# A trunk kernel on one Trainium2 core: another order in its plain norm tiles, its passage to attention as a step list, and a softmax that takes the query latent's root

## The chip, the cores and the metric

The kernel runs on one core of one Trainium2 chip. The metric is the device time of one execution in microseconds (us).

## The reference

Two layers on x of 1024 tokens by 1024 features: layer 0 mixes by a short gated convolution, layer 1 by multi-head latent attention, and both end in a squared-ReLU MLP. Every sublayer has a norm before it and one behind it:

```python
h = modulate(rmsnorm(x, norm_g[l, 0]), sh_m, sc_m)
y = short_conv_mixer(...) if l < N_A else mla_mixer(...)
x = x + g_m[:, None, :] * rmsnorm(y, norm_g[l, 1])
h = modulate(rmsnorm(x, norm_g[l, 2]), sh_f, sc_f)
x = x + g_f[:, None, :] * rmsnorm(squared_relu_mlp(h, w_up, w_down), norm_g[l, 3])
# attention, 8 heads; c_kv and k_pe are made once from x after layer 0
c_kv = rmsnorm(kv_a[..., :256], kv_a_norm_g); k_pe = apply_rope(kv_a[..., 256:], cos, sin)
q = rmsnorm(h @ q_a_w, q_a_norm_g) @ q_b_w      # 384 latent channels, per head 128 + 64 rotary
s = (qn @ k_nope.T + qp @ k_pe.T) / sqrt(192)   # masked by chunks of 64, then softmax, then @ v
```

## The kernel before, in words

A float32 product is three fp32r matmuls of a high and a low part (`mm`, L168 to L170), and `split_w` (L172 to L174) makes the parts: ACT copies the high part, DVE subtracts for the low one. A matmul is 128x128 by 128x512.

**Seams.** Where a sublayer ends, its down product comes as eight tiles of 128 tokens by 1024 features, 24 matmuls each, into one of two 128x1024 PSUM tiles (`big`). `Seam.tile` (L309 to L317) adds a tile to y (DVE), squares and sums it (ACT, L255), takes the root (ACT L257, DVE L262), scales (DVE L315), adds to x (DVE L316), stores x (L317), and squares the new x; `flush` (L295, ACT) makes the pre-norm for the next product. The sequence on each engine is pinned to the written one. At three places a seam stands between stages: behind the convolution (about 344 to 392 us of the trace), behind the first MLP (from 977.6 us), behind attention (1467 to 1516 us). The first and third write five plain tiles and run the rest by a hand-written list, `ORDER`, in which the transposes for the next product (L418), their splits (L429, L430) and its first matmuls are mixed with the last tiles. The last seam of the kernel keeps its order in both kernels.

**Passage to attention** (977.6 to 1116.1 us). All eight tiles are plain ones. `h_steps` transposes the pre-normed tokens (PE L484), scales them (ACT L486) and splits them (DVE L490, L491). `first_block` multiplies half the tokens by the query latent's weights; `latent` (L1311 to L1321) copies each product out of PSUM, squares it, sums over channels with a 128x512 product against ones (L1315), takes root and reciprocal of all 128x512 sums (L1316, L1317), scales by it and by the gain (L1319) and splits. It is done for both halves of the query latent and both of the key latent; `rotary_keys` makes the rotary key.

**Attention** (1116.1 to 1467 us, heads from 1160). Per head come eight score tiles (`scores`, 128 queries by up to 1024 keys): matmuls into `big` (L1471), a mask (L1472), the negated row maximum (DVE L1474), Exp with the maximum as bias and a running sum (ACT L1477), reciprocal (L1481), scaling (L1482), transposes and splits of the probabilities (`turn`, L1497 to L1501) and the products with the values. Ahead of the first head stand `queries`, `rotary` and `keys` for both halves. Background steps (`run_bg`, modulation vectors, DVE L195) are spread over it; outside the pinned stretches a scheduler orders the engines.

## Time and profile before

| | |
|---|---|
| median of 3 runs | 2141.66 us (2141.5 to 2142.57) |
| the profiled execution | 2144.59 us, its span 2142.8 us |
| granted TensorE clock, mean | 0.996 |
| busy: PE, PEld, DVE, ACT | 97%, 80%, 72%, 49% |
| seam behind the convolution, 344.6 to 391.8 us | PE busy 45.59 of 47.2 us |
| passage, 977.6 to 1116.1 us | PE busy 131.5 of 138.5 us |
| start of attention, 1116.1 to 1160 us | PE busy 38.78, DVE 41.49 of 43.9 us |
| heads, 1160 to 1412 us | PE busy 243.93, DVE 193.35 of 252 us |

PE is TensorE's matmuls and PEld its weight loads, which overlap them; DVE is VectorE, ACT ScalarE. A row of the timeline is start, duration, engine, line, operation, the tiles written and read, and in brackets the idle time before it with the engine that ended it. A busy PE is not PE at its peak, since pipelined matmuls overlap.

### The profile page before, as it was taken

What the parts mean: (1) busy time and instruction counts of PE and PEld (TensorE: products, weight loads), DVE (VectorE), ACT (ScalarE), POOL (GpSimd) and SP (SyncE); (2) the same over time, 40 slices, a digit from 0 to 9 for tenths busy, and PEclk for the clock granted to TensorE, in tenths of its full rate; (3) what the DMA queues carried; (4) which work ended last, traced back from release to release, by engine and by line L of the source; (5) the groups of instructions that cost most, each with busy time, mean ns of one, the idle gap of its engine ahead of it and who ended that gap; (6) DMA issues with size and microseconds to landing.
All of it is one profiled execution on the core that took longest, in us unless ns stands there. A gap on an engine that the chain in (4) does not pass through costs nothing.

```text
span 2142.8 us, 25254 instructions
## 1 busy us (share of the span) xinstructions
PE 2083.0 (97%) x9638; PEld 1715.1 (80%) x9638; DVE 1532.3 (72%) x2066; ACT 1060.5 (49%) x1512; POOL 4.0 (0%) x8
## 2 busy tenths in 40 slices
PE   5999999999999999999899999999999999999998
PEld 4888888888888878888777878877888888888887
DVE  5877776977665668876788877766977665558556
ACT  4533353845444434344665555564845444444342
POOL 0000000000000000000000000000000000000000
PEclk9999999999999999999999999999999999999999
DMA  8344454466443976465214231043455543853343
GB/s 245 95 147 146 131 200 136 133 192 215 157 152 131 326 230 226 151 210 178 81 59 124 78 106 44 26 149 132 129 184 184 183 166 134 300 191 122 98 147 138
DMA packets 242336, 330.85 MB, mean 154 GB/s; under 512 B 18630, under 2 KB 143907, under 8 KB 242215
## 3 DMA queue, kind: packets, MB, share of 16 engines
q1 hardware_dynamic: 204328, 248.57, 37.2%
q10 hardware_dynamic: 37886, 80.67, 10.0%
q8 instruction: 76, 1.25, 0.2%
q14 instruction: 46, 0.37, 0.0%
HBM read 248.45 MB, written 80.74 MB: 154 GB/s over the span
## 4 chain that ended last, share of the span: by engine, by line
PE 75%; DVE 12%; ACT 6%; DMA 5%; issue 2%; ACTq 0%; SPq 0%; DVEq 0%
PE one L170 40%; PE mm L170 19%; PE tp L170 7%; PE big L170 3%; ACT junk L255 2%; DMA raw<-in_ada_w_dram 2%; PE big L1471 2%; DVE y L315 1%; DVE raw L316 1%; DVE acc L195 1%; PE tp L1497 1%; DVE small L1474 1%; DVE y L309 1%; DVE pt L1501 1%; ACT small L257 1%
## 5 line engine op out<-in xcount | busy, mean ns | idle before, releaser
L170 PE MATMUL one<-slot,uphi 128*128 128x512 f32 x1240 | 381.9, 389 | 0.0
L170 PEld LDWEIGHTS one<-slot,uphi 128*128 128x128 f32 x1240 | 232.8, 188 | 48.7 <-issue 0.5
L170 PE MATMUL big<-slot 128*128 128x512 f32 x1152 | 267.6, 392 | 0.9 <-DVE slot L174 0.6
L170 PEld LDWEIGHTS big<-slot 128*128 128x128 f32 x1152 | 216.0, 189 | 47.7 <-ACT y L924 1.0
L170 PE MATMUL one<-slot,uplo 128*128 128x512 f32 x620 | 243.0, 392 | 1.6 <-DVE y L584 1.6
L173 ACT ACTIVATE ring<-w 128x1024 fp32r<-128x1024 f32 x98 | 103.8, 1059 | 267.1 <-PE tp L170 145.7
L170 PE MATMUL one<-ring,ring 128*128 128x512 f32 x1008 | 229.5, 389 | 0.3 <-DVE ring L174 0.3
L170 PEld LDWEIGHTS one<-ring,ring 128*128 128x128 f32 x1008 | 189.2, 188 | 40.0 <-DVE ring L174 0.7
L174 DVE TENSOR_TENSOR ring<-w,ring 128x1024 fp32r<-128x1024 f32 x98 | 119.8, 1222 | 122.8 <-ACT ring L173 122.6
L174 DVE TENSOR_TENSOR uplo<-raw,uphi 128x1024 fp32r<-128x1024 f32 x117 | 142.7, 1222 | 79.1 <-ACT uphi L173 79.0
L173 ACT ACTIVATE uphi<-raw 128x1024 fp32r<-128x1024 f32 x117 | 123.7, 1059 | 136.1 <-PE one L170 77.4
L170 PE MATMUL mm<-ring,ring 128*128 128x512 f32 x672 | 163.1, 391 | 2.4 <-DVE ring L174 2.4
L170 PE MATMUL tp<-ring,ring 128*128 128x512 f32 x672 | 161.8, 389 | 0.0
L170 PE MATMUL mm<-slot,uphi 128*128 128x512 f32 x504 | 157.9, 394 | 0.5 <-DVE slot L430 0.5
L170 PEld LDWEIGHTS mm<-ring,ring 128*128 128x128 f32 x672 | 125.6, 188 | 29.7 <-DVE ring L174 3.5
L170 PEld LDWEIGHTS tp<-ring,ring 128*128 128x128 f32 x672 | 126.1, 188 | 26.2
L170 PEld LDWEIGHTS one<-slot,uplo 128*128 128x128 f32 x620 | 116.4, 188 | 26.5 <-DVE y L584 2.4
L195 DVE SCALAR_TENSOR_TENSOR acc<-raw,csil,acc 128x1024 f32<-128x1024 f32 x88 | 112.4, 1277 | 35.1 <-DMA raw<-in_ada_w_dram 32.5
L174 DVE TENSOR_TENSOR ring<-raw,ring 128x1024 fp32r<-128x1024 f32 x98 | 119.3, 1218 | 10.7 <-ACT ring L173 10.7
L170 PE MATMUL one<-slot,s 128*128 128x512 f32 x468 | 114.0, 393 | 0.7 <-DVE s L174 0.7
L170 PEld LDWEIGHTS mm<-slot,uphi 128*128 128x128 f32 x504 | 94.8, 189 | 21.1 <-issue 1.4
L582 ACT ACTIVATE y<-one 128x512 f32<-128x512 f32 x62 | 36.7, 592 | 143.5 <-PE one L170 114.3
(272 smaller groups left out, 3487.0 us busy)
## 6 DMA issues: line engine op xcount, KB each, us to landing
ha<-y ACTq DMA_DIRECT2D x196, 256.0 KB, 3.0
raw<-ha SPq DMA_DIRECT2D x98, 512.0 KB, 4.3
raw<-in_ada_w_dram SPq DMA_DIRECT2D x80, 512.0 KB, 4.4
raw<-in_mlp_up_w_dram SPq DMA_DIRECT2D x70, 512.0 KB, 4.9
w<-in_mlp_down_w_dram SPq DMA_DIRECT2D x56, 512.0 KB, 4.8
raw<-hd SPq DMA_DIRECT2D x24, 512.0 KB, 4.3
xs<-raw ACTq DMA_DIRECT2D x24, 512.0 KB, 3.1
raw<-xs SPq DMA_DIRECT2D x24, 512.0 KB, 4.2
```

What stands on the lines that cost most here:

```text
L170: nc.tensor.matmul(out_, lhs[a], rhs[b], start=first and i == 0, stop=last and i == 2, skip_group_check=more)
L173: nc.scalar.activation(hi, src, AF.Copy)
L174: nc.vector.tensor_tensor(lo, src, hi.bitcast(F32), op=ALU.subtract)
L195: nc.vector.scalar_tensor_tensor(acc, raw, s, acc, op0=ALU.mult, op1=ALU.add)
L255: nc.scalar.activation(junk, src, AF.Square, accum_out=ss)
L257: nc.scalar.activation(rt, ss, AF.Sqrt, bias=eps_d)
L309: nc.vector.tensor_tensor(y, y, p_, op=ALU.add)
L315: nc.vector.scalar_tensor_tensor(y, y, rroot(ss), self.gmb, op0=ALU.mult, op1=ALU.mult)
L316: nc.vector.tensor_tensor(xr, xr, y, op=ALU.add)
L582: nc.scalar.activation(dst, x_, AF.Copy)
L1471: nc.tensor.matmul(o_, a, m_, start=j == 0, stop=j == 4)
L1474: nc.vector.tensor_reduce(mx, sp[:, :n], AX.X, ALU.max, negate=True)
```

## The change

1. **Plain tiles.** `Seam.tile` adds, squares y, then does the x addition, store and square of the *previous* tile, scales its own tile, and last makes the previous tile's pre-norm. The two list-run seams have it in their first five tiles.
2. **Passage.** `LATENTS`, a list of named steps in pinned order, takes the place of `h_steps`, `first_block`, `latent` and `rotary_keys`: the last three tiles of the seam (`mm5`, `add5` ...), transposes (`tr`), scaling (`tu`), splits (`sp`), blocks of the query product (`f`, `g`, `e`), the key product (`v`, `k`). Query products of the second half lie in `big`.
3. **Query latent's root.** It is no longer multiplied into the latent. The squares are summed with 128x1 products against ones into a column per 128 tokens, `rsq`, with sqrt(192) folded in; the gain is applied where the product leaves PSUM. `scores` multiplies the negated maximum by `rsq` (a 128x1 DVE instruction, 64 in all) and gives it to Exp as scale.
4. **Key latent's root.** Also from 128x1 products, root and reciprocal on 128x4, then spread over 128x512 by four transposes of a broadcast column.
5. **Start of attention.** Keys of half 0 and values 0 and 1 are written ahead of the queries of half 0; `run_bg(5)` is written as 0 for head 0.
6. The epsilons lie in one 128x8 tile; masked scores are -2^120.

```diff
 SLOTS = 6
 AHEAD = 5
+LATENTS = """
+mm5 tr0_0 tr0_1 add5 tu0_0 mm6 tu0_1 sq5 sp0_0 sp0_1 stt5 tr0_2 rc4 xad5 tr0_3 pre4 mm7 add6 tu0_3 dma5 tu0_2 sp0_3
+sq6 sp0_2 sqx5 stt6 tr0_4 rc5 xad6 pre5 tr0_5 f0 add7 tu0_5 dma6 sqx6 sp0_5 tr0_6 f1 mul7 sq7 rc6 pre6 f2 stt7 tu0_4
...
 """.split()
 VEC_ROWS = 109
@@ -152,10 +166,11 @@
     ones = cp.tile([P, P], F32, name="ones")
     nc.vector.memset(ones, 1.0)
-    eps_d = cp.tile([P, 1], F32, name="eps_d")
-    nc.vector.memset(eps_d, D * EPS)
-    eps_1 = cp.tile([P, 1], F32, name="eps_1")
-    nc.vector.memset(eps_1, EPS)
+    eps = cp.tile([P, 8], F32, name="eps")
+    eps_d, eps_1, eps_q = (eps[:, i:i + 1] for i in range(3))
+    for e, v in ((eps_d, D * EPS), (eps_1, EPS), (eps_q, (NOPE + ROPE) * EPS)):
+        nc.vector.memset(e, v)
+    rsq = cp.tile([P, NT], F32, name="rsq")
     nc.scalar.activation(small(), eps_1, AF.Sqrt)
     vecs = cp.tile([P, VEC_ROWS], F32, name="vecs")
...
         def flush(self):
             if self.rest is not None:
-                y, xr, ss = self.rest
-                nc.scalar.activation(y, xr, AF.Copy, scale=rroot(ss))
+                t, y, xr = self.rest
+                nc.vector.tensor_tensor(xr, xr, y, op=ALU.add)
+                nc.scalar.dma_start(self.xdst[t * P:(t + 1) * P, :], xr)
+                self.ss = None if self.last else squares(self.nx, xr)
+        def tail(self):
+            if self.rest is not None and not self.last:
+                t, y, xr = self.rest
+                nc.scalar.activation(y, xr, AF.Copy, scale=rroot(self.ss))
             self.rest = None
-        def tile(self, t, p_, steps):
+        def tile(self, t, p_):
             y = self.ys[t]
             if t == 0:
                 return
             with pinned():
                 nc.vector.tensor_tensor(y, y, p_, op=ALU.add)
-                self.back()
                 ss = squares(self.nx, y)
+                if not self.last:
+                    self.flush()
+                nc.vector.scalar_tensor_tensor(y, y, rroot(ss), self.gmb, op0=ALU.mult, op1=ALU.mult)
+                self.tail()
+                self.rest = (t, y, xr)
+                if self.last:
+                    self.flush()
+        def acts(self, first):
+            with pinned():
                 self.flush()
-                if t >= 5:
-                    self.front(steps, 2)
-                nc.vector.scalar_tensor_tensor(y, y, rroot(ss), self.gmb, op0=ALU.mult, op1=ALU.mult)
-                nc.vector.tensor_tensor(xr, xr, y, op=ALU.add)
-                nc.scalar.dma_start(self.xdst[t * P:(t + 1) * P, :], xr)
-                if not self.last:
-                    self.rest = (y, xr, squares(self.nx, xr))
-        def acts(self, first):
-            acts, ss, sx, rs = {}, {}, {first - 1: self.rest[2]}, {}
+            acts, ss, sx, rs = {}, {}, {first - 1: self.ss}, {}
             self.load(first + 2)
...
-    def h_steps(tp, ys, half, key, dst):
...
-    def first_block(seam, steps0, steps1, ws, h):
...
-    def latent(h, hf, ws, g, dst, steps=None, firsts=None):
...
-    def rotated(p_, hf, scale, stab, z, y):
+    def rotated(p_, hf, stab, z, y):
         sl = slice(hf * HALF, (hf + 1) * HALF)
         for i in range(4):
             j = i ^ 1
-            nc.scalar.activation(y[32 * i:32 * i + 32, :], p_[32 * j:32 * j + 32, :], AF.Copy, scale=scale)
-        nc.vector.scalar_tensor_tensor(z, p_, scale, ctab[:, sl], op0=ALU.mult, op1=ALU.mult)
+            nc.scalar.activation(y[32 * i:32 * i + 32, :], p_[32 * j:32 * j + 32, :], AF.Copy)
+        nc.vector.tensor_tensor(z, p_, ctab[:, sl], op=ALU.mult)
         nc.vector.tensor_tensor(y, y, stab[:, sl], op=ALU.mult)
...
+    def latents(seam, ws, ys):
+        acts = seam.acts(PLAIN)
...
+        def turn(fam, hf, k):
+            p_ = tp_ps()
+            for t in range(4):
+                nc.tensor.transpose(p_[:, t * P:(t + 1) * P], ys[hf * 4 + t][:, k * P:(k + 1) * P], ident)
+            t_[fam, k] = p_
...
+        def rooms(hf):
+            if hf == 0:
+                t_["big"] = big_ps()
+                return [mm_ps(), mm_ps(), t_["big"][:, :HALF]]
+            return [t_["big"][:, HALF:], *halves(big_ps())]
+        def block(hf, k):
+            if k == 0:
+                out_[hf] = rooms(hf)
+            for p_, w in zip(out_[hf], ws):
+                part_of(p_, w, hf, k)
+        def rest(m):
+            for k in range(4, KD):
+                part_of(out_[1][m], ws[m], 1, k)
...
+        def q_high(hf, m):
+            nc.scalar.activation(qaT[0][:, m, half(hf)], out_[hf][m], AF.Copy, scale=gq[:, m:m + 1])
+        def q_low(hf, m):
+            nc.vector.scalar_tensor_tensor(qaT[1][:, m, half(hf)], out_[hf][m], gq[:, m:m + 1], qaT[0][:, m, half(hf)].bitcast(F32),
+                                           op0=ALU.mult, op1=ALU.subtract)
+        def q_square(hf, m):
+            nc.scalar.activation(sq_of(hf, m), out_[hf][m], AF.Square)
+        def add_squares(key):
+            a, b = t_["sq", key]
+            nc.vector.tensor_tensor(a, a, b, op=ALU.add)
+        def token_sums(p_, sq):
+            for t in range(4):
+                nc.tensor.matmul(p_[:, t:t + 1], sq[:, t * P:(t + 1) * P], ones[:, 0:1], start=True, stop=True)
...
+        def q_sums(hf):
+            p_ = t_["qs", hf] = big_ps() if hf else mm_ps()
+            token_sums(p_, t_["sq", hf][0])
+        def q_root(hf):
+            nc.scalar.activation(rsq[:, 4 * hf:4 * hf + 4], t_["qs", hf][:, :4], AF.Sqrt, scale=(NOPE + ROPE) / QL, bias=eps_q)
...
+        def q_inverse(hf):
+            nc.vector.reciprocal(rsq[:, 4 * hf:4 * hf + 4], rsq[:, 4 * hf:4 * hf + 4])
...
+        def k_product(hf, m):
+            p_ = out_["k", hf, m] = big_ps()[:, :HALF] if m == 2 else mm_ps()
+            for k in range(KD):
+                part_of(p_, wk[m], hf, k)
...
+        def k_sums(hf):
+            p_ = t_["vs", hf] = big_ps()
+            token_sums(p_, t_["sq", "k", hf][0])
...
+        def k_root(hf):
+            rs = t_["vr", hf] = small(4)
+            nc.scalar.activation(rs, t_["vs", hf][:, :4], AF.Sqrt, scale=1.0 / KL, bias=eps_1)
...
+        def k_spread(hf):
+            for t in range(4):
+                nc.tensor.transpose(t_["vs", hf][:, HALF + t * P:HALF + (t + 1) * P], t_["vr", hf][:, t:t + 1].to_broadcast([P, P]), ident)
+        def k_norm(hf, m):
+            a = t_["raw", hf][m]
+            nc.vector.scalar_tensor_tensor(a, a, gk[:, m:m + 1], t_["vs", hf][:, HALF:], op0=ALU.mult, op1=ALU.mult)
...
+        with pinned():
+            for name in LATENTS:
+                acts[name]()
+        return t_["qw"], t_["kw"]
+    qw_, kw = latents(seam, ws, ys)
...
     def queries(Q, qw_, hf):
         p_ = project(qw_, slice(0, P), qaT, 3, hf)
         Q[hf] = part(at, "q", 3, [P, HALF])
-        nc.scalar.activation(Q[hf][0], p_, AF.Copy, scale=SM)
-        nc.vector.scalar_tensor_tensor(Q[hf][1], p_, SM, Q[hf][0].bitcast(F32), op0=ALU.mult, op1=ALU.subtract)
+        nc.scalar.activation(Q[hf][0], p_, AF.Copy)
+        nc.vector.tensor_tensor(Q[hf][1], p_, Q[hf][0].bitcast(F32), op=ALU.subtract)
     def rotary(R, qw_, hf, room=mm_ps):
         z, y = (at.tile([P, HALF], F32, tag="z" + i, name=nm("z"), bufs=b) for i, b in (("a", 2), ("b", 1)))
-        rotated(project(qw_, slice(P, 256), qaT, 3, hf, room), hf, SM, stab, z, y)
+        rotated(project(qw_, slice(P, 256), qaT, 3, hf, room), hf, stab, z, y)
         R[hf] = [at.tile([P, HALF], F32R, tag="r", name=nm("r"), bufs=4) for _ in range(2)]
         for i, t_ in enumerate(R[hf]):
...
         nc.vector.memset(sp[:CHUNK, n - CHUNK:n], MASKED)
         mx = small()
         nc.vector.tensor_reduce(mx, sp[:, :n], AX.X, ALU.max, negate=True)
+        rs = rsq[:, i:i + 1]
+        nc.vector.tensor_tensor(mx, mx, rs, op=ALU.mult)
         pt = at.tile([P, n], F32, tag=f"p{i}", name=nm("p"), bufs=1)
         l_ = small()
-        nc.scalar.activation(pt, sp[:, :n], AF.Exp, bias=mx, accum_out=l_)
+        nc.scalar.activation(pt, sp[:, :n], AF.Exp, scale=rs, bias=mx, accum_out=l_)
                 nc.scalar.dma_start(hd[self.h][:, self.hf * HALF:(self.hf + 1) * HALF], o_)
     K, Q, R, V = {}, {}, {}, {}
-    for hf in (1, 0):
-        queries(Q, qw_, hf)
-        rotary(R, qw_, hf, tp_ps)
-        keys(K, kw, 0, hf)
+    queries(Q, qw_, 1)
+    rotary(R, qw_, 1, tp_ps)
+    keys(K, kw, 0, 0)
+    for b in range(2):
+        values(V, kw, b)
+    queries(Q, qw_, 0)
+    rotary(R, qw_, 0, tp_ps)
+    keys(K, kw, 0, 1)
     before, kw0 = None, kw
     for h in range(H):
         more = h + 1 < H
@@ -1544,21 +1663,19 @@
         r_ = {hf: R[hf][h % 2] for hf in range(2)}
         raw_q = load_q_b(h + 1) if more else None
         raw_kv = load_kv_b(h // 2 + 1) if more and h % 2 else None
-        run_bg(5)
+        run_bg(5 if h else 0)
         pts = {}
         pts[7], end = scores(7, K, Q, r_)
         if before:
             before.turn(2)
         else:
-            values(V, kw0, 0)
-            values(V, kw0, 1)
+            values(V, kw0, 2)
         end()
         pts[6], end = scores(6, K, Q, r_)
         if before:
             before.turn()
             before.mul(3)
         else:
-            values(V, kw0, 2)
             values(V, kw0, 3)
         end()
         pts[5], end = scores(5, K, Q, r_)
```

On DVE, in the seam behind attention, rows of the second and third plain tile before (`y` the tile, `big` its product, `raw` x, `small` a column):

```order
L309 TENSOR_TENSOR y_11582<-y_11582,big_11949 128x1024
L262 RECIPROCAL small_11982<-small_11947 128x1
L262 RECIPROCAL small_11985<-small_11980 128x1
L315 SCALAR_TENSOR_TENSOR y_11582<-y_11582,small_11985,gmb_8467 128x1024
L316 TENSOR_TENSOR raw_11929<-raw_11929,y_11582 128x1024
L309 TENSOR_TENSOR y_11583<-y_11583,big_11995 128x1024
L262 RECIPROCAL small_12028<-small_11993 128x1
L262 RECIPROCAL small_12031<-small_12026 128x1
```

and now:

```order
L321 TENSOR_TENSOR y_11651<-y_11651,big_12011 128x1024
L300 TENSOR_TENSOR raw_11996<-raw_11996,y_11650 128x1024
L277 RECIPROCAL small_12051<-small_12042 128x1
L325 SCALAR_TENSOR_TENSOR y_11651<-y_11651,small_12051,gmb_8833 128x1024
L277 RECIPROCAL small_12054<-small_12049 128x1
L321 TENSOR_TENSOR y_11652<-y_11652,big_12057 128x1024
L300 TENSOR_TENSOR raw_11998<-raw_11998,y_11651 128x1024
L277 RECIPROCAL small_12097<-small_12088 128x1
```

The addition to x (`raw`) of a tile now stands behind the next tile's first addition, and the root for the previous tile's pre-norm, which came ahead of the tile's own root, now comes behind its scaling.

On PE, in the passage, where the second half's query products go from the second to the third 128 channels (`slot` the split tokens, `uphi`/`uplo` weights, `tp` a transpose's result):

```order
L170 MATMUL mm_7906<-slot_6940,uphi_7242 128x512
L170 MATMUL mm_7934<-slot_6940,uplo_7249 128x512
L170 MATMUL mm_7934<-slot_7218,uphi_7248 128x512
L170 MATMUL mm_7934<-slot_6940,uphi_7248 128x512
L484 MATMUL tp_7938<-cs,y_5386 128x128
L484 MATMUL tp_7938<-cs,y_5387 128x128
L484 MATMUL tp_7938<-cs,y_5388 128x128
L484 MATMUL tp_7938<-cs,y_5389 128x128
L170 MATMUL mm_7934<-slot_6940,uplo_7249 128x512
```

and now, where the second half begins:

```order
L1319 MATMUL tp_7852<-cs,y_5394 128x128
L185 MATMUL big_7662<-slot_6941,uplo_7245 128x512
L185 MATMUL big_7662<-slot_7219,uphi_7244 128x512
L185 MATMUL big_7662<-slot_6941,uphi_7244 128x512
L185 MATMUL big_7858<-slot_6941,uplo_7251 128x512
L185 MATMUL big_7858<-slot_7219,uphi_7250 128x512
L185 MATMUL big_7858<-slot_6941,uphi_7250 128x512
L185 MATMUL big_7858<-slot_6941,uplo_7257 128x512
L185 MATMUL big_7858<-slot_7219,uphi_7256 128x512
L185 MATMUL big_7858<-slot_6941,uphi_7256 128x512
L1319 MATMUL tp_7876<-cs,y_5387 128x128
```

The product that took a third `mm` tile behind two others now lies in `big`, and the three run side by side through the channels of h.

On DVE, at the first score tile (`acc` is a background step, `v` the values, `p` the probabilities):

```order
L1472 MEMSET big_8484 64x64
L1455 TENSOR_TENSOR v_8514<-mm_8501,v_8514 128x512
L1474 TENSOR_REDUCE small_8496<-big_8484 128x1
L1455 TENSOR_TENSOR v_8530<-mm_8517,v_8530 128x512
L1472 MEMSET big_8536 64x64
L195 SCALAR_TENSOR_TENSOR acc_8469<-raw_8837,csil,acc_8469 128x1024
L174 TENSOR_TENSOR kw_8958<-raw_8835,kw_8957 128x1024
L1481 RECIPROCAL small_8533<-small_8499 128x1
```

and now:

```order
L1568 TENSOR_TENSOR v_8535<-mm_8522,v_8535 128x512
L1587 TENSOR_REDUCE small_8516<-big_8504 128x1
L1585 MEMSET big_8541 64x64
L1589 TENSOR_TENSOR small_8516<-small_8516,rsq 128x1
L1568 TENSOR_TENSOR v_8572<-mm_8559,v_8572 128x512
L210 SCALAR_TENSOR_TENSOR acc_8835<-raw_8847,csil,acc_8835 128x1024
L210 SCALAR_TENSOR_TENSOR acc_8835<-raw_9302,csil,acc_8835 128x1024
L1596 RECIPROCAL small_8538<-small_8520 128x1
L1587 TENSOR_REDUCE small_8553<-big_8541 128x1
L1597 TENSOR_SCALAR p_8519<-p_8519,small_8538 128x1024
```

The factor's product with `rsq` stands between reduction and Exp; of the first five background steps, four stood ahead of the first reduction and now three do.

More of the change, by code (lines that the diff above doesn't have):

```diff
@@ L918, in down @@
             seam.products = products
-            for t in range(PLAIN if f == nf and steps is None else NT):
+            for t in range(PLAIN if f == nf and not seam.last else NT):
                 p_ = products(t)
                 if f == nf:
-                    seam.tile(t, p_, steps)
+                    seam.tile(t, p_)
                 elif f == n_rows and not begun:
@@ L1292, in trunk_kernel @@
     ctab = pp.tile([P, S], F32, name="ctab")
+    ckT = [pp.tile([P, 2, S], F32R, name=f"ckT{i}") for i in range(2)]
+    qaT = [slots[i][:, 0:3, :] for i in range(2)]
+    kk = [slots[i][:, 3, :] for i in range(2)]
+    up, ws, seam = down_phase(slots, (ROWS,), mlp_down_w[0], from_dram(hd), "g0f", xs[0], xs[1], q_a_w[0], "1m", ys=ys, pairs=False)
     ld(ctab, consts[:, C_T:C_T + S])
[L1294 to L1323 removed]
+    def rotated(p_, hf, stab, z, y):
         sl = slice(hf * HALF, (hf + 1) * HALF)
@@ L1630, in trunk_kernel @@
     banks(False)
[L1631 removed]
+    down(slots, (ROWS,), mlp_down_w[1], from_dram(hd), ys, Seam(nx, ys, vtile["g1f"], xs[2], out[0], last=True), 0,
          begun=True)
```

230 lines of the change are left out of this document (122 added, 108 removed).

## The prediction

> **What bounds the kernel now.** I read the page's busy times and its chain first.
>
> ```profile
> PE 2083.0 (97%) x9638; PEld 1715.1 (80%) x9638; DVE 1532.3 (72%) x2066; ACT 1060.5 (49%) x1512; POOL 4.0 (0%) x8
> PE 75%; DVE 12%; ACT 6%; DMA 5%; issue 2%; ACTq 0%; SPq 0%; DVEq 0%
> ```
>
> PE is busy 97% of the span, and three quarters of the chain that ended last is PE. So only two things can pay: matmul work that goes, and time in which PE waits. That time lies in stages, so I next cut the busy times by stage.
>
> ```profile
> core 0: us, PE busy (x) PEld busy (x) DVE busy (x) ACT busy (x) POOL busy (x), PEclk, DMA share, GB/s
> 344.60:391.80 47.20, 45.59 (x214) 37.12 (x213) 35.37 (x49) 32.03 (x58) 0.00 (x0) 1.00 0.52 175
> 977.60:1027.00 49.40, 45.99 (x209) 37.34 (x207) 35.14 (x44) 27.57 (x50) 0.00 (x0) 1.00 0.48 170
> 1027.00:1034.20 7.20, 5.91 (x26) 4.72 (x26) 7.06 (x11) 5.92 (x10) 0.00 (x0) 0.76 0.46 146
> 1034.20:1116.10 81.90, 79.63 (x385) 62.88 (x384) 63.84 (x91) 47.67 (x72) 0.00 (x0) 1.00 0.18 53
> 1116.10:1160.00 43.90, 38.78 (x202) 31.03 (x201) 41.49 (x69) 28.02 (x50) 0.96 (x1) 1.00 0.43 134
> 1160.00:1412.00 252.00, 243.93 (x1375) 203.24 (x1374) 193.35 (x402) 141.05 (x285) 0.00 (x0) 1.00 0.19 62
> 1467.80:1516.20 48.40, 45.42 (x214) 37.06 (x213) 35.33 (x49) 33.30 (x59) 0.00 (x0) 1.00 0.51 169
> ```
>
> Row by row: the seam behind the convolution, the passage (three rows, 138.5 us), the start of attention, the heads, the seam behind attention. PE has gaps in each. Only at the start of attention is DVE nearly full (41.49 of 43.9 us): there DVE sets the pace, everywhere else PE does, or a chain that passes through all three engines. What PE needs without waiting comes from unbroken pieces of the chain:
>
> ```profile
> 1098.24 13.42 PE mm L170 x59
> 1084.29 0.44 PE tp L484 x4
> 1078.62 1.09 PE tp L1315 x2
> 1239.60 1.84 PE L214 MATMUL mm<-ones,acc 128*128 128x1 f32 x16
> ```
>
> A 512-column matmul takes 13.42/59 = .2275 us, a transpose .11, a product against ones 1.09 (two records each), and a product with one column 1.84/8 = .23 (the last row is eight of them, also two records each).
>
> **The plain tiles.** Now a tile of the seam behind attention, on DVE and, in the third row, ACT:
>
> ```profile
> 1480.61 1.21 DVE L309 TENSOR_TENSOR y<-y,big 128x1024 f32<-128x1024 f32 x1
> 1481.10 1.06 ACT L255 ACTIVATE junk<-raw 128x1024 bf16<-128x1024 f32 x1 [2.14 <-DVE raw L316]
> 1482.48 1.04 ACT L255 ACTIVATE junk<-y 128x1024 bf16<-128x1024 f32 x1
> 1483.98 0.16 DVE L262 RECIPROCAL small<-small 128x1 f32<-128x1 f32 x1 [1.20 <-ACT small L257]
> 1484.18 1.29 DVE L315 SCALAR_TENSOR_TENSOR y<-y,small,gmb 128x1024 f32<-128x1024 f32 x1
> 1485.50 1.22 DVE L316 TENSOR_TENSOR raw<-raw,y 128x1024 f32<-128x1024 f32 x1
> 1486.64 1.21 DVE L309 TENSOR_TENSOR y<-y,big 128x1024 f32<-128x1024 f32 x1
> ```
>
> From one addition (L309) to the next it takes 1486.64 - 1480.61 = 6.03 us, while PE makes a tile in 24 x .2275 = 5.46. The ring is: add, then ACT squares the *previous* x before it squares y, then root, scale, x addition, next add. So each tile falls .57 us further behind PE, and PE pays when the lists of the two seams take over:
>
> ```profile
> 372.68 0.53 PEld L418 LDWEIGHTS tp<-cs,y 128*128 128x128 f32 x5 [0.67 <-ACT y L295]
> 388.36 0.19 PEld L170 LDWEIGHTS mm<-slot,uplo 128*128 128x128 f32 x1 [1.22 <-DVE slot L429]
> 389.08 0.30 PEld L170 LDWEIGHTS mm<-slot,uphi 128*128 128x128 f32 x2 [0.54 <-DVE slot L430]
> 1497.09 0.53 PEld L418 LDWEIGHTS tp<-cs,y 128*128 128x128 f32 x5 [1.95 <-ACT y L295]
> 1512.77 0.19 PEld L170 LDWEIGHTS mm<-slot,uplo 128*128 128x128 f32 x1 [1.30 <-DVE slot L429]
> 1513.50 0.30 PEld L170 LDWEIGHTS mm<-slot,uphi 128*128 128x128 f32 x2 [0.54 <-DVE slot L430]
> ```
>
> After the change ACT squares y directly behind the add. By the rows above, add 1.21, square to reciprocal 1483.98 - 1482.48 = 1.50, to the scaling .20, scaling 1.29: 4.2 us, under 5.46, so PE's cadence holds and the lag goes. The work is the same; the x addition, its store (issued on ACT's queue), the second square and the pre-norm move one tile back and fill the gaps. The pre-norm of tile 4, which the list's transposes wait for, is then the late one: it now needs the x addition, square, root and copy after tile 4's scaling, but starts about four lags (2.3 us) earlier. Behind the convolution the waits are .67 + 1.22 + .54 = 2.4 us: between -0.7 (only the first goes) and -2.4 (all). I take **-1.8**. Behind attention 1.95 + 1.30 + .54 = 3.8: between -2.0 and -3.8. I take **-2.7**. Both lie somewhat past the middle, since the later waits are on DVE's splits, which the same lag delayed.
>
> **The passage.** 480 matmuls (8 tiles of 24; 144 and 96 for the latents, 48 for the rotary key) x .2275 = 109.2, 128 transposes x .11 = 14.1 and four products against ones = 4.4 make 127.7 us of need in 138.5: waits of 10.8. The largest:
>
> ```profile
> 1027.05 1.53 PEld L484 LDWEIGHTS tp<-cs,y 128*128 128x128 f32 x8 [3.70 <-ACT tt L486]
> 1033.07 0.43 PEld L484 LDWEIGHTS tp<-cs,y 128*128 128x128 f32 x4 [1.66 <-ACT tt L486]
> 1066.53 0.19 PEld L170 LDWEIGHTS mm<-slot,uplo 128*128 128x128 f32 x1 [2.44 <-ACT lat L1311]
> L1317 DVE RECIPROCAL sq<-sq 128x512 f32<-128x512 f32 x4 | 13.4, 3352 | 5.9 <-ACT sq L1316 5.9
> ```
>
> The first two come where the eight plain tiles end: transposes wait for pre-norms that lag as above. The third is the second half's third product, queued for the `mm` tile that ACT has not yet copied out. After the change the last three tiles are mixed with transposes, the second half's products lie in `big`, and the four reciprocals of 3.35 us leave DVE, so that splits no longer stand behind them. What PE then needs: 109.2 + 14.1 + 16 column products x .23 = 3.7 + 8 transposes = .9, together 127.9. DVE loses 13.4 of its 106.0 us there (35.14 + 7.06 + 63.84) and is some 71% busy, so it has room; six copies out of PSUM go from ACT, since gain and split now read PSUM. What waits remain no row shows, as the list has not run. From below, .5 us; from above, the waits of the list-run seam behind the convolution, 2.4 in 47.2 us, which over 138.5 us would be 7.1. That seam's waits are for the most part the plain tiles' lag, which goes here too, so I take 2.5, nearer the lower end. 127.9 + 2.5 - 138.5 = **-8.1**, between -3.5 and -10.1. SP's loads are the same in number; the key weights and rotary tables are issued earlier, behind tile 4, in a stretch whose DMA share is .48.
>
> **The start of attention.** DVE paces it, and it gets eight multiplications of 128x1 (below), while the splits that lose their constant factor keep their size; the background steps stand where they stood but for one, since the scheduler takes them forward although 0 is written. The values ahead of the second queries give DVE other work, not less. At the least it gains DVE's idle 43.9 - 41.49 = 2.4; at the most it loses eight full handovers of .28 (worked out next), 2.2. I take **+1.0**, near DVE's own added work, 8 x .147 = 1.2.
>
> **The heads.** Each of 64 score tiles gets a DVE instruction between reduction and Exp, and Exp gets its scale as a column.
>
> ```profile
> L1012 DVE TENSOR_TENSOR sh<-tp,bias x8: 147/148/150, 25.1 to 74.1; 128x1 f32<-128x1 f32 x8
> L295 ACT ACTIVATE y<-raw,small x16: 1132/1138/1149, 353.4 to 1495.9; 128x1024 f32<-128x1024 f32 x16
> L173 ACT ACTIVATE uphi<-raw x117: 1039/1061/1067, 90.0 to 1805.7; 128x1024 fp32r<-128x1024 f32 x117
> ACT p L1477 <- DVE small L1474: 34.7, 27, 2.2
> PEld mm L170 <- DVE pt L1501: 9.1, 22, 1.3
> ```
>
> Such a product takes .148 us; a copy with a scale column takes 1.138 against 1.061 without, so .077 more. Over the 56 tiles of this window: .225 x 56 = 12.6 us if all of it came through, nothing if PE's other work covers it. Exp does wait for the reduction in 27 of these tiles (fourth row), so the chain is often the late one for ACT, and queued behind Exp there, and behind the factor on DVE, are the halves of the turned probabilities, for which the weight loads wait 22 times already (last row). But PE waits only 252.0 - 243.93 = 8.1 us in all, 3%, with heads interleaved so that values of the last head fill score gaps. I take a quarter, **+3.0**.
>
> **The rest.** The epsilon tile and the masked value change operands, not instructions, and lie off every wait above: 0.
>
> **The sum.** -1.8 - 8.1 + 1.0 + 3.0 - 2.7 = -8.6 against the profiled execution's 2144.59: 2136.0. The median is 2.93 lower, so 2141.66 - 8.6 = **2133.0**.
>
> **A rule weighed: the clock.**
>
> ```profile
> 1029.21 1.05 PE L170 MATMUL mm<-slot,uphi 128*128 128x512 f32 x2
> 1066.87 0.62 PE L170 MATMUL mm<-slot,uphi 128*128 128x512 f32 x2
> 1412.73 3.29 PE L170 MATMUL big<-slot 128*128 128x512 f32 x7 [0.63 <-DVE slot L174]
> ```
>
> Behind the 3.7 us gap of the passage two matmuls took 1.05 us, at a granted clock of .76 in that row of stages; behind the 2.4 us gap .62, full speed; yet seven at 1412.73 took 3.29 us instead of 7 x .2275 = 1.6, with .63 us of idle ahead of them. The slow ones of the passage lie in its waits already. The Trainium skill, "TensorE: Matmul & The Clock Gate", Part 1, says that the clock halves after an idle window of about 3.4 us and that the window runs free of the program. By that rule the first two rows agree; the third only fits if the window's phase counts, and a program of another length may lose or keep it: 1.7 us, so the sum would be -10.3 by the rule at its best and -8.6 by the row.
>
> **Rivals.** (a) *Slower: the softmax factor lies wholly on the chain.* From a small DVE instruction to the next is 1484.18 - 1483.98 = .20, with the .077 makes .277, times 64 = 17.7 us against gains of 12.6: +5.1, **2146.8**. It decides from 12.6/64 = .197 us per tile. For it: the 27 waits of Exp. Against: PE idles only 3% there. Chance .08. (b) *The passage's waits only move*, into the ring of two `tp` and two `tt` tiles or the list's in-order engines; the change then does not do what it says. Passage between 0 and -3.5, the rest as above: -0.5 to -4.0, about **2139.5**. For it: the list-run seams do wait. Against: the largest waits have named causes that are taken away. Chance .17. (c) *The additions hide*: heads and start free, the waits all gone, -2.4 - 10.1 - 3.8 = -16.3, **2125.4**. For it: PE, at 97%, covers the heads. Chance .15.
>
> **Numbers.** My forecast, 2129 to 2137.4, has .60. The measurement can tell about 0.2%, 4.3 us. Faster: .60 + .15 = .75; within: .17; slower: .08. The range leaves out (a) and a little beyond (b) and (c): 2125.0 to 2141.5.
>
> **What would show it.** Plain additions 5.5 us apart; no PE wait on the pre-norm behind them; under 3 us of waits in the passage, now about 130 us; Exp's waits up by about .2 in some tiles while PE's idle in the heads grows by 3 us. Wrong if the list keeps gaps over 1 us at `tt` or at the roots, or if the heads are over 6 us longer.

## The result, and the profile after

| | before | changed |
|---|---|---|
| median of 20 runs each | 2141.58 us (2136.64 to 2145.01) | 2136.32 us (2130.03 to 2142.74) |
| ratio | | 0.9977, 95% interval 0.9967 to 0.9987 |
| profiled execution | 2144.59 us | 2140.12 us |

The change is faster by 0.23% (0.13 to 0.33), 5 us, where 8.6 were forecast. The two profiled executions differ by 4.5 us. The page of the changed kernel, busy times and chain:

```profile
PE 2084.1 (97%) x9670; PEld 1723.4 (81%) x9670; DVE 1518.7 (71%) x2125; ACT 1064.4 (50%) x1506; POOL 4.0 (0%) x8
PE 80%; DVE 10%; ACT 4%; DMA 4%; issue 1%; SPq 0%; ACTq 0%; DVEq 0%
```

PE does the same work, and more of the chain is PE: 80% in place of 75%. To see where the rest lies, I cut both traces at the same instructions: first product of the stage behind the convolution up to the first of the MLP; first down product of the MLP's last chunk up to the first query product (the passage); from there to the last values of head 0 (the start); to the first attention down product (the heads); to the next MLP. Busy times by stage before (columns as in the table of stages of the prediction):

```profile
295.10:391.50 96.40, 94.67 (x429) 77.26 (x428) 63.96 (x74) 52.37 (x79) 0.00 (x0) 1.00 0.56 183
977.50:1116.10 138.60, 131.63 (x617) 105.04 (x616) 106.05 (x145) 81.16 (x131) 0.00 (x0) 0.99 0.30 100
1116.10:1162.40 46.30, 41.18 (x217) 33.00 (x216) 43.05 (x73) 29.22 (x52) 0.96 (x1) 1.00 0.40 127
1162.40:1412.70 250.30, 241.63 (x1361) 201.27 (x1359) 192.48 (x400) 140.55 (x286) 0.00 (x0) 1.00 0.20 63
1412.70:1515.90 103.20, 100.11 (x450) 81.31 (x451) 66.49 (x79) 58.50 (x88) 0.00 (x0) 0.98 0.55 179
```

and in the changed kernel:

```profile
296.00:389.80 93.80, 93.75 (x428) 77.43 (x427) 63.73 (x73) 53.36 (x79) 0.00 (x0) 1.00 0.56 183
975.00:1105.50 130.50, 128.23 (x645) 106.85 (x644) 90.32 (x138) 76.70 (x125) 0.96 (x1) 1.00 0.33 109
1105.50:1154.10 48.60, 42.11 (x221) 34.85 (x221) 43.12 (x80) 29.11 (x52) 0.00 (x0) 0.96 0.35 110
1154.10:1411.90 257.80, 245.54 (x1363) 204.37 (x1361) 195.49 (x457) 146.82 (x286) 0.00 (x0) 0.99 0.20 62
1411.90:1511.50 99.60, 99.39 (x450) 81.35 (x451) 66.35 (x79) 59.60 (x88) 0.00 (x0) 0.98 0.57 186
```

Read the second column, the length of each stage: -2.6, -8.1, +2.3, +7.5, -3.6, together -4.5. The three stages that were to gain did, as sized or better; the attention (start and heads) took back 9.8 us of 14.3. The plain tiles of the changed kernel, on DVE behind attention:

```profile
1477.46 1.22 DVE L321 TENSOR_TENSOR y<-y,big 128x1024 f32<-128x1024 f32 x1 [0.95 <-PE big L185]
1482.90 1.22 DVE L321 TENSOR_TENSOR y<-y,big 128x1024 f32<-128x1024 f32 x1 [0.95 <-PE big L185]
1488.34 1.22 DVE L321 TENSOR_TENSOR y<-y,big 128x1024 f32<-128x1024 f32 x1 [0.90 <-PE big L185]
```

Additions stand 5.44 us apart, and now DVE waits for PE. What was left for PE to wait for, in the weight loads of the two list-run seams and of the passage:

```profile
372.72 0.53 PEld L430 LDWEIGHTS tp<-cs,y 128*128 128x128 f32 x5 [0.28 <-ACT y L307]
387.66 0.30 PEld L185 LDWEIGHTS mm<-slot,uphi 128*128 128x128 f32 x2 [0.32 <-DVE slot L442]
1008.14 0.53 PEld L1319 LDWEIGHTS tp<-cs,y 128*128 128x128 f32 x5 [0.28 <-ACT y L307]
1047.90 0.19 PEld L185 LDWEIGHTS big<-slot,uplo 128*128 128x128 f32 x1 [0.71 <-ACT sq L1365]
1067.42 0.42 PEld L1319 LDWEIGHTS tp<-cs,y 128*128 128x128 f32 x4 [2.36 <-ACT tt L1325]
1494.12 0.53 PEld L430 LDWEIGHTS tp<-cs,y 128*128 128x128 f32 x5 [0.29 <-ACT y L307]
1509.09 0.30 PEld L185 LDWEIGHTS mm<-slot,uphi 128*128 128x128 f32 x2 [0.35 <-DVE slot L442]
1511.11 0.42 PEld L430 LDWEIGHTS tp<-cs,y 128*128 128x128 f32 x4 [0.38 <-ACT q L434]
```

That is .6 us behind the convolution in place of 2.4, and 1.0 behind attention in place of 3.8. In the passage these gaps add up to 3.4 us. The 10.8 of before were worked out as length less need; in the same way it is now 130.5 - 127.9 = 2.6. In the heads, see what Exp waits for and what PE waits for from Exp (us in total, times, longest); first the changed kernel, then the second of these rows before:

```profile
ACT p L1592 <- DVE small L1589: 42.8, 41, 2.6
PE big L1584 <- ACT p L1592: 6.1, 8, 1.4
```

```profile
PE big L1471 <- ACT p L1477: 1.1, 2, 0.7
```

Exp now waits 41 times for DVE in place of 27, and PE waits 5 us more for Exp to free a score tile's PSUM. And there is a new gap at the start, with slow matmuls behind it:

```profile
1117.71 2.53 PE L185 MATMUL mm<-w,ckT 128*128 128x256 f32 x12 [2.50 <-DVE k L1538]
1120.04 2.95 PE L185 MATMUL mm<-slot,w 128*128 128x512 f32 x9
```

The values, now written ahead of the second queries, wait 2.5 us for the key's split to free their PSUM tile, and of the matmuls behind it twelve run slowly, .213 us from start to start at 256 columns and .427 at 512: the last eight products of the values and the first four of the nine behind them. The nine take 2.95 us; nine of the same size at 1112.99 took 2.23. Stages below are therefore also given **net**: each sequence of three or more matmuls at double duration is found in the trace, and what it is over full speed is taken off. The attention (start and heads) is 296.6 us before, all net; 306.4 with the change, of it 2.8 slow (1.5 at the start, 1.3 in the heads), 303.6 net.

### The profile page after: what moved, and what is told of

It reads as the page before. It is cut to its first block, busy times and chain, and to the rows that moved or that the text cites. A ratio compares the mean times of both kernels' runs of the same rounds, so it can differ in the third digit from the quotient of the medians.

```text
span 2138.3 us, 25363 instructions
## 1 busy us (share of the span) xinstructions
PE 2084.1 (97%) x9670; PEld 1723.4 (81%) x9670; DVE 1518.7 (71%) x2125; ACT 1064.4 (50%) x1506; POOL 4.0 (0%) x8
## 4 chain that ended last, share of the span: by engine, by line
PE 80%; DVE 10%; ACT 4%; DMA 4%; issue 1%; SPq 0%; ACTq 0%; DVEq 0%
PE one L185 38%; PE mm L185 18%; PE big L185 11%; PE tp L185 7%; DMA raw<-in_ada_w_dram 3%; PE big L1584 2%; DVE acc L210 1%; ACT junk L270 1%; PE tp L1612 1%; ACT z L1270 1%; DVE small L1587 1%; PE tp L1319 1%; DVE y L321 1%; DVE p L1597 0%; DVE raw L300 0%
## 5 line engine op out<-in xcount | busy, mean ns | idle before, releaser
L210 DVE SCALAR_TENSOR_TENSOR acc<-raw,csil,acc 128x1024 f32<-128x1024 f32 x88 | 112.0, 1273 | 34.1 <-DMA raw<-in_ada_w_dram 32.2
L185 PE MATMUL mm<-slot,uphi 128*128 128x512 f32 x424 | 131.0, 390 | 0.0
L185 PEld LDWEIGHTS one<-slot,s 128*128 128x128 f32 x468 | 88.6, 189 | 19.4 <-DVE s L189 0.9
```

What stands on the lines that cost most here:

```text
L185: nc.tensor.matmul(out_, lhs[a], rhs[b], start=first and i == 0, stop=last and i == 2, skip_group_check=more)
L210: nc.vector.scalar_tensor_tensor(acc, raw, s, acc, op0=ALU.mult, op1=ALU.add)
```

## The experiments

My theory after the comparison: the factor lies on the chain reduction, product, Exp, on which PE now waits. Rival: the start's new order. Each ratio below is to the kernel before, run beside it. The runs come from three sets on different chips, so whole times are best compared by their ratios. Stages come from one trace of each run.

**Without the factor.**

```diff
-        nc.vector.tensor_tensor(mx, mx, rs, op=ALU.mult)
-        nc.scalar.activation(pt, sp[:, :n], AF.Exp, scale=rs, bias=mx, accum_out=l_)
+        nc.scalar.activation(pt, sp[:, :n], AF.Exp, bias=mx, accum_out=l_)
```

> The changed kernel without the query root's factor in the scores: no 128x1 product, and Exp without a scale column (so the query latent's root is left out of the result). Theory (the factor lies on the chain reduction, product, Exp, and PE waits for it): from the first query product to the attention's down product, 306.4 us with the change and 296.6 before, falls to 296 to 299, and PE's waits for Exp from 6.1 to about 1 us; total 7 to 10 us under the change. Rival (the new order at the attention's start shifts heads and background steps against each other): the stretch stays above 303 us and the total within 3 us of the change.

Measured: 2130.86 us, ratio 0.9958 (0.9944 to 0.9971). Start and heads:

```profile
1101.70:1149.30 47.60, 42.74 (x221) 35.02 (x221) 42.27 (x75) 28.91 (x55) 0.00 (x0) 0.96 0.37 112
1149.30:1401.00 251.70, 243.74 (x1361) 202.52 (x1359) 191.03 (x398) 141.79 (x285) 0.00 (x0) 0.99 0.21 63
```

299.3 us, 296.2 net: 7.4 under the change, at the level of before. PE's waits for Exp in the heads fall from 6.1 to 2.3 us. The whole time falls by less than the 7 to 10 us expected: 5.5 by the medians, 4.1 by the two ratios.

**The start as before, the factor kept.** The order of queries, keys and values is the old one, and, not in the cut below, `run_bg` is written as 5 again for head 0.

```diff
-    queries(Q, qw_, 1)
-    rotary(R, qw_, 1, tp_ps)
-    keys(K, kw, 0, 0)
-    for b in range(2):
-        values(V, kw, b)
-    queries(Q, qw_, 0)
-    rotary(R, qw_, 0, tp_ps)
-    keys(K, kw, 0, 1)
+    for hf in (1, 0):
+        queries(Q, qw_, hf)
+        rotary(R, qw_, hf, tp_ps)
+        keys(K, kw, 0, hf)
```

> The changed kernel with the start of attention written as before (queries, rotary and keys for both halves, then the values inside head 0, five background steps written ahead of head 0). Theory of the factor: only the start changes, 48.6 us to about 46 to 49, and the heads stay at 255 to 258 us; total within 3 us of the change. Rival (the start's order is what the attention lost): the whole stretch falls from 306.4 to 300 us or less.

Measured: 2134.57 us, 0.9966 (0.9954 to 0.9979).

```profile
1104.10:1150.60 46.50, 41.59 (x222) 33.53 (x221) 38.57 (x79) 29.74 (x54) 0.00 (x0) 1.00 0.24 72
1150.60:1405.10 254.50, 242.94 (x1362) 201.49 (x1360) 194.56 (x454) 146.58 (x285) 0.00 (x0) 1.00 0.20 62
```

301.0 us with no slow sequence: between the two expectations. 2.6 net of the loss, and the slow matmuls, go with this edit: .6 at the start, 2.0 in the heads. But it changes two things. Of the eight background steps that the change has at the start, four now run in the passage; busy time of L210, passage and start, first in the change, then in this run:

```profile
975.00:1105.50 130.50, 0.00 (x0) 1.00 0.33 109
1105.50:1154.10 48.60, 10.14 (x8) 0.96 0.35 110
```

```profile
973.60:1104.10 130.50, 5.13 (x4) 1.00 0.38 125
1104.10:1150.60 46.50, 5.12 (x4) 1.00 0.24 72
```

The passage takes them for nothing (130.5 us in both). What the values' order costs by itself isn't shown.

**The plain order alone, in the kernel before.** `tile` of the two list-run seams does the x addition, store and square of the previous tile behind its own square of y, nothing else.

> The kernel before with nothing but the new order of the five plain tiles in the two list-run seams (behind the convolution, behind attention). Theory: tiles come every 5.44 us, the two stages lose 2.6 and 3.6 us as in the trace of the change, everything else stays: 6 us under before, so that this part alone gives more than the whole change (5 us). Rival (the gain of these stages needs the rest, or is given back in the next stage): under 4 us.

Measured: 2136.55 us, 0.9974 (0.9963 to 0.9984).

```profile
295.40:389.30 93.90, 93.85 (x429) 77.35 (x429) 63.71 (x72) 53.28 (x79) 0.00 (x0) 1.00 0.57 181
972.30:1112.60 140.30, 134.26 (x618) 106.79 (x617) 106.20 (x145) 81.26 (x131) 0.00 (x0) 0.96 0.30 98
1409.00:1508.30 99.30, 99.07 (x450) 81.66 (x451) 66.37 (x77) 59.69 (x87) 0.00 (x0) 0.98 0.56 181
```

-2.5 and -3.9 us, and the old passage (here with 2.8 us of slow matmuls) between them. So a few lines give 4.9 us by the medians, 5.6 by the ratio, where the whole change gives 5.3 and 4.9: its passage and its attention nearly cancel. 6 were expected.

**The root spread in the passage, no factor.** The query latent is kept in float32 until its root is there; the root is spread by transposes, as for the key latent:

```diff
+        def q_spread(hf):
+            for t in range(4):
+                nc.tensor.transpose(t_["qs", hf][:, t * P:(t + 1) * P], rsq[:, 4 * hf + t:4 * hf + t + 1].to_broadcast([P, P]), ident)
+        def q_norm(hf, m):
+            nc.vector.tensor_tensor(qraw[hf][:, m, :], qraw[hf][:, m, :], t_["qs", hf][:, :HALF], op=ALU.mult)
```

> The changed kernel with the query latent's root spread in the passage as the key latent's is (eight more transposes, six more 128x512 copies on ACT, six 128x512 products on DVE in place of none), and scores without a factor, as before; the whole computation is done. Theory of the factor: the passage grows from 130.5 us to 131 to 134, the attention falls from 306.4 to 296 to 300: 4 to 9 us under the change, 9 to 14 under before. Rival of the start's order: attention stays above 303 us and the total is at or above the change.

Measured: 2133.01 us, 0.9960 (0.9947 to 0.9972); passage 133.5, attention 299.5 us, 297.2 net. (Other than that text says, one of six low parts was made ahead of its high part, so the query latent of this run is not the right one; the instructions are the same.) The theory holds in the stages: 3 us more in the passage, 6.4 net less in the attention. In the whole it is 3.3 us under the change and 8.5 under before, just short of the 4 to 9 and 9 to 14 expected.

Next the factor by its parts.

**Product alone, scale alone, product off the chain.**

```diff
 # product only
+        nc.vector.tensor_tensor(mx, mx, ones[:, 0:1], op=ALU.mult)
 # scale only
+        nc.scalar.activation(pt, sp[:, :n], AF.Exp, scale=ones[:, 0:1], bias=mx, accum_out=l_)
 # product off the chain: in end(), behind Exp
+            nc.vector.tensor_tensor(small(), mx, rsq[:, i:i + 1], op=ALU.mult)
```

> The changed kernel with the 128x1 product between reduction and Exp, but by a column of ones, and Exp without a scale column (so the root is left out). Attention net of slow-clock matmuls was 303.6 us with the change and 296.2 without the factor. Theory of the chain by its parts (.148 us product with its handover, .077 scale column): 300.5 to 302 net, two thirds of the 7.4 us. Rival (the scale column is what costs, since Exp is what PE waits for): 297 to 299 net.

> The changed kernel without the product, Exp with a scale column of ones (so the root is left out). Theory of the chain by its parts: 298 to 299.5 us net of slow matmuls, one third of the 7.4 us. Rival (the scale column is what costs): 301 to 303.5 net.

> The changed kernel with the same 64 products of 128x1 moved behind Exp, ahead of the reciprocal, into a column that nobody reads, and Exp without a scale column (so the root is left out). Same work on DVE. Theory of the chain (what counts is where the product stands): 296 to 298.5 us net of slow matmuls, at or little above the run without a factor. Rival of load (what counts is DVE's time, wherever it stands): 300 us or more, as with the product on the chain.

| | median us, ratio (interval) | attention, us and net us |
|---|---|---|
| product only | 2137.07, 0.9983 (0.9970 to 0.9996) | 304.9, 302.9 |
| scale only | 2133.88, 0.9964 (0.9952 to 0.9977) | 303.8, 301.7 |
| product off the chain | 2136.23, 0.9969 (0.9953 to 0.9984) | 302.2, 300.3 |
| both (the change) | 2136.32, 0.9977 (0.9967 to 0.9987) | 306.4, 303.6 |

The theory by parts falls: of 7.4 us the product alone brings 6.7 and the scale alone 5.5, and even a product that nobody waits for brings 4.1. Parts that add up to far more than the whole have something in common. One such thing is the order: the scheduler orders the unpinned attention anew for each of these kernels (against the change's order, some 80 to 96 of PE's rows stand elsewhere without the factor, with the scale alone or with the product off the chain, and 32 with the product alone). But order isn't all: the run with the product off the chain has nearly the order of the run without the factor (9 rows of PE, 17 of DVE and 2 of ACT stand elsewhere) and is 4.1 us longer. It met the figure of its rival, that DVE's added time counts wherever it stands, and that rival is not excluded. By whole times these four can't be told apart, as their intervals overlap. So I held every engine's order in the attention by added dependencies without semaphores.

**The same order, with and without.**

```diff
+    for e_, order_ in FIXED.items():
+        made = [i for i in nc.cur_bb.bb.instructions[n0_:] if str(i.engine).endswith(e_)]
+        order_ = [int(x) for x in order_.split()]
+        for a_, b_ in zip(order_, order_[1:]):
+            tc.add_manual_dep(made[b_], made[a_].name, NO_SYNC, reason="fixed")
```

> The changed kernel without the factor in the scores (product gone, Exp without a scale column, so the root is left out), but with every engine's order in the attention held at what the changed kernel has. The runs so far each had an order of their own, as the scheduler orders anew when an instruction goes. Theory of the factor's own time: attention net of slow matmuls 296 to 298.5 us (303.6 with the change). Rival (the scheduler's other order makes the difference, not the instruction): 301 us or more.

> The changed kernel in its own order with the product (by a column of ones) but Exp without a scale column (so the root is left out). By the durations, .148 with its handover and .077, the product should have two thirds of what the factor costs: if the run without both is 296 to 298.5 us net, then 300.5 to 302. Rival (either one alone costs nearly all, as in the runs with free orders): 302.5 or more.

> The changed kernel with the whole factor, its product directly behind the reduction, in the order that the scheduler gave the kernel without a factor; the whole computation is done. Theory of the factor's own time: 302 to 305 us net, as with the change, since the order matters little. Rival of the order: 296 to 299 us, as without a factor.

Attention, us net of slow matmuls:

| | order of the change | order of the kernel without factor |
|---|---|---|
| no factor | 300.2 | 296.2 |
| product only | 302.0 | |
| product and scale | 303.6 | 303.8 |

In the traces of the three held runs, PE's rows stand in the order they were held to. Heads without the factor and with the product alone, in the change's order:

```profile
1155.20:1408.20 253.00, 242.89 (x1362) 202.99 (x1360) 190.26 (x400) 142.32 (x286) 0.00 (x0) 0.99 0.20 62
```

```profile
1152.10:1407.90 255.80, 243.60 (x1362) 202.92 (x1360) 195.09 (x457) 141.97 (x286) 0.00 (x0) 0.99 0.20 62
```

Start and heads with the factor, in the order of the kernel without it:

```profile
1103.50:1152.40 48.90, 42.96 (x223) 35.18 (x222) 43.45 (x83) 29.39 (x53) 0.00 (x0) 0.97 0.36 109
1152.40:1409.20 256.80, 245.54 (x1358) 201.61 (x1356) 199.69 (x452) 146.05 (x283) 0.00 (x0) 0.99 0.20 61
```

Without the factor, 300.2 lies between both expectations. In the change's order the factor costs 3.4 us, 1.8 for the product and 1.6 for the scale; the other 4.0 of the 7.4 are an order that the scheduler found only for the kernel without it. Given that better order, the kernel with the factor gains nothing (303.8): there the factor costs 7.6. How fine such a reading is, two pairs of traces tell that have the same attention in the same order. The runs without the factor and with the root in the passage have 296.2 and 297.2 us net. The kernel before and the run with the plain order alone have 296.6 and 296.4 as they stand, though the second holds about 1.5 us of slow matmuls and the first none. So 3.4, 4.0 and 7.6 are clear of that, and the split into 1.8 and 1.6 isn't shown. In medians: 2134.55 (0.9969, 0.9958 to 0.9980), 2135.57 (0.9974, 0.9965 to 0.9984), 2140.99 (0.9998, 0.9988 to 1.0008). By the ratios the factor costs 1.7 us in the change's order, where the intervals overlap, and 8.6 in the other, where they don't. The last median is 4 us above the change's, which its trace's stages don't show; that stays open.

**The key root as before,** in the changed kernel: one product against ones, root and reciprocal on 128x512.

```diff
-            token_sums(p_, t_["sq", "k", hf][0])
+            nc.tensor.matmul(p_[:, :HALF], ones, t_["sq", "k", hf][0], start=True, stop=True)
```

> The changed kernel with the key latent's root made as before (one 128x512 product against ones, root and reciprocal on 128x512, 3.35 us each on DVE, no transposes). Theory that the list made the passage's gain and DVE has room there: passage within 1 us of 130.5, and at most 2 us more at the start of attention, where the second half's root ends. Rival (the small roots made much of the gain): passage and start together 4 us or more longer.

Measured: 2141.06 us, 0.9999 (0.9990 to 1.0009). Passage, start and heads:

```profile
973.60:1103.20 129.60, 127.33 (x629) 105.38 (x628) 93.48 (x138) 76.62 (x125) 0.95 (x1) 1.00 0.34 110
1103.20:1154.00 50.80, 43.38 (x217) 35.94 (x216) 45.93 (x80) 30.19 (x53) 0.00 (x0) 0.93 0.35 105
1154.00:1413.10 259.10, 245.72 (x1362) 204.38 (x1360) 196.08 (x457) 146.59 (x286) 0.00 (x0) 0.99 0.20 61
```

The passage is even .9 us shorter (PE does less there), the start 2.2 longer, about as the theory has it; but the heads are 1.3 longer too, and the median loses 4.7 us by the two ratios, more than the trace's 2.6. What of that is order wasn't tried. By this run the small key root gains nothing in the passage, where DVE has room, but in what DVE carries into the attention: 2.8 us more of DVE's time stand at the start (45.93 for 43.12).

**The version that beats both**: the root in the passage, no factor, the old start.

> The changed kernel with the query latent's root spread in the passage (as in the earlier run, with one low part now made behind its high part) and the start of attention as before; the whole computation is done. By the stages of the earlier traces: passage 133 to 134 us, attention 296 to 299, so some 10 to 13 us under before (2129 to 2132 beside 2141.5) and 5 to 8 under the change. Rival (the old start costs again without the factor, or the passage and the start collide): attention above 300 us and no better than 2133.

Measured: **2126.76 us**, 0.9928 (0.9915 to 0.9942). Passage, start and heads:

```profile
975.00:1108.20 133.20, 130.54 (x654) 108.89 (x652) 98.35 (x148) 79.58 (x132) 0.95 (x1) 0.99 0.38 122
1108.20:1151.50 43.30, 39.80 (x221) 33.21 (x220) 38.24 (x69) 28.51 (x52) 0.00 (x0) 1.00 0.26 78
1151.50:1402.30 250.80, 242.27 (x1364) 201.94 (x1361) 192.53 (x400) 140.48 (x286) 0.00 (x0) 1.00 0.20 63
```

At the start DVE is no longer full (38.24 of 43.3 us, before 43.05 of 46.3), and no slow sequence is left in the attention. Better than expected: 294.1 us. The start is 3 us under before, and DVE does 4.8 us less there. The trace shows where that went: as in the run with the old start, four of the eight background steps, 5.1 us of DVE's time, now run in the passage, where they cost nothing that shows. That this makes the 3 us wasn't tested by itself.

## Why the prediction was right, and where it was off

- **The sum**: -8.6 forecast, -5.3 measured. 2136.32 lies in the forecast, near its upper end, and some of that is luck: the two seams and the passage gave 1.7 us more than the 12.6 forecast, the attention took 5.8 more than the 4.0, and the two errors have opposite signs.
- **What bounds the kernel** held: the gain came in the named stages, and PE's busy time as a whole did not move (2083.0, 2084.1). By stage it did: 3.4 us less in the passage, 4.8 more at the start and in the heads.
- **Plain tiles**: -1.8 and -2.7 forecast, -2.6 and -3.6 measured, the first just past its bound of 2.4 and the second near 3.8, and the run with that order alone has -2.5 and -3.9. The cadence is the forecast one. I took a middle where all waits had one cause.
- **The passage**: -8.1 forecast, -8.1 measured, with 2.6 us of waits left, by the prediction's own reckoning, for the 2.5 assumed, and no slow matmuls. The hit is closer than its reasons: 2.5 was picked between .5 and 7.1. PE's idle time fell from 7.0 to 2.3 us and its busy time from 131.6 to 128.2, which the sum does not part. The one wait of 2.4 us is the `tt` gap that was named as a mark of error. That DVE has room there is right (90.32 of 130.5 us). With the query root spread in the passage it is 133.5 us, so some 5 of the 8.1 stay without that move; the run with the old key root shows none of it coming from the small one.
- **The start**: +1.0 forecast, +2.3 measured, .8 net of 1.5 us of slow matmuls. The step "the values ahead of the second queries give DVE other work, not less" overlooked that the values wait 2.5 us for the PSUM tile that the key's split frees. That wait was not in the sum, and the slow matmuls stand right behind it. The step "the background steps stand where they stood" held (eight at the start in both kernels), but the runs with the old start show four of them running in the passage.
- **The heads**: +3.0 forecast, +7.5 measured, about 6.2 net. That they are over 6 us longer was the other named mark of error. The step that failed is "I take a quarter", as a price for the whole. The mechanism is right (Exp waits 41 times for 27, PE for Exp 6.1 us for 1.1), but the sum has one order in mind. In the change's own order the factor costs 3.4 us over start and heads, near that quarter of 12.6; in the order of the kernel without it 7.6. The term that was missing is the 4.0 us of an order that the kernel with the factor does not profit from. I read PE's small idle share as cover. That it was small because the order had been fitted to the shorter chain would explain both prices; it is argued from them, not shown.
- **The scale column** was sized at .077 us from a copy. In the traces Exp on 128x1024 takes 1.117 us before and 1.208 with the column: .091.
- **The rival of the softmax factor** was the right one to fear. It decides from 12.6 us of loss; start and heads lost 9.8, and 7.0 net.
- That `run_bg(0)` changes nothing was not tested alone.

## What to carry to other kernels

A 128x1 instruction on a chain that every score tile passes is not priced by its .15 us, and not by the idle share of the engine that ends last: hold the order and take the instruction out. Where a scheduler orders the code, an experiment that removes an instruction removes an order as well; two runs in one held order tell the two apart, and the price may still differ from order to order. A small vector that would be applied 64 times in the tight stage can be cheaper applied once, in bulk, in a stage that has room: 3 us in the passage for 6 in the attention.

## What the runs showed of the hardware

The same kernel's runs differ by 12.7 us (2130.03 to 2142.74), and the granted clock goes with it: at .998 2130.0 us, at .997 2131.0 to 2136.3, at .994 2136.9 to 2141.9, at .991 2140.9 and 2142.7 (.995 and .996 lie between and overlap). Slow matmuls don't need a long gap. The wait at the same place of the passage, first in the changed kernel, then in the run with the root in the passage:

```profile
1067.42 0.66 PE L1319 MATMUL tp<-cs,y 128*128 128x128 f32 x4 [1.94 <-ACT tt L1325]
1068.15 0.62 PE L185 MATMUL mm<-slot,uphi 128*128 128x512 f32 x2
```

```profile
1067.85 0.66 PE L1320 MATMUL tp<-cs,y 128*128 128x128 f32 x4 [2.45 <-ACT tt L1326]
1069.69 1.05 PE L185 MATMUL mm<-slot,uphi 128*128 128x512 f32 x2
```

After 1.94 us pairs take .62, after 2.45 us 1.05, about half speed, for seven matmuls. It isn't the length alone that decides. Here is one wait in the kernel before and in the run with the plain order alone:

```profile
1066.53 0.50 PE L170 MATMUL mm<-slot,uplo 128*128 128x512 f32 x1 [2.02 <-ACT lat L1311]
1066.87 0.62 PE L170 MATMUL mm<-slot,uphi 128*128 128x512 f32 x2
```

```profile
1061.32 0.50 PE L170 MATMUL mm<-slot,uplo 128*128 128x512 f32 x1 [2.04 <-ACT lat L1332]
1061.66 1.02 PE L170 MATMUL mm<-slot,uphi 128*128 128x512 f32 x2
```

And in the run without the factor nine score matmuls from 1346.10 on ran at half speed, with no idle time over .23 us in the 10 us ahead of them. The slow sequence at the start of the attention's down product, weighed in the prediction, is there in the changed kernel and gone in the runs with the old start and with the root in the passage (97.6 and 97.9 us for that stage in place of 99.6). The Trainium skill, "TensorE: Matmul & The Clock Gate", Part 1, says that the window over which activity is watched runs free of the kernel. By that the same gap may cost in one run and not in another, which agrees with 2.02 and 2.04 us above. Its length of 3.4 us of idling before the clock falls does not fit gaps of 2.0 to 2.5 us. The Trainium skill, "ScalarE: Activation LUTs", What ACT_TABLE_LOAD costs, puts each 128x1 pointer operand at about .093 us; Exp's .091 agrees.
